# Attention maxima from q's high part alone: one 128-row product per query tile becomes two 64-row products in the two halves of TensorE's rows

## The chip, the cores and the metric

The kernel is one program on one core of a Trainium2 chip. Its engines run side by side, each with its own instruction stream in a fixed order, and they wait for each other through semaphores: TensorE (matrix products; PE in the profile, with its weight loads shown apart as PEld), VectorE (DVE), ScalarE (ACT), GpSimd (POOL) and SyncE (SP, which issues most DMAs). The metric is the device time of one execution in microseconds (us). Lower is better.

## The reference

One layer of a bidirectional hybrid encoder is applied to 2048 prompt positions and, with the same weights, to 256 sample positions (width 1024). What matters here is the attention half of the mixer: 8 query heads over 2 key/value heads, head width 64.

```
def block(qi):
    s = jnp.einsum('bqhgd,bkhd->bhgqk', qi, k).astype(jnp.float32) * scale
    p = jax.nn.softmax(s, axis=-1)
    return jnp.einsum('bhgqk,bkhd->bqhgd', p.astype(v.dtype), v)
```

q and k are RMS-normed per head and rotated before that. Next to attention there is an 8-head mLSTM (also bidirectional); then `x + [mLSTM; attention] @ w_out`, a second RMSNorm, `w_up`, a width-3 depthwise convolution, `silu(g) * a`, `w_down`, and a final RMSNorm. A softmax does not depend on the number that is subtracted from its scores, as long as it is the same for all keys of a query and near enough to their maximum that the exponentials stay in range.

## The kernel before, in words

The work runs in four phases. Phase A projects q, k, v of attention and the gates (lines 138 to 332). Then attention (`attention`, line 427) and the mLSTM (`mlstm`, line 614) run interleaved; when the mLSTM is done, the output projection (`phase_c`, line 879) takes its place beside attention. Phase D (line 1071) is the feed-forward part.

Precise products are made from pieces: a number is split into a high part (type fp32r) and the low remainder, and a product is high x high + high x low + low x high. For attention the pieces are stacked in the 128 rows (partitions) that TensorE contracts over:

- `kk` (128 rows x 512 keys): k's high part in rows 0 to 63, and the same high part once more in rows 64 to 127 (line 458 loads it twice).
- `qq` (128 rows x 512 queries): q's high part in rows 0 to 63, q's low part in rows 64 to 127.
- `kl1` (65 rows): k's low part, and a row of ones. `qm` (65 rows): q's high part, and a row that takes minus the query's maximum.

So `kk` against `qq` gives k_high x (q_high + q_low), and `kl1` against `qm` adds k_low x q_high minus the maximum.

Attention goes over 36 head blocks (`hbs`). A large one is one head and 4 tiles of 128 queries against all 2048 keys (32 of them); a small one is two heads of the sample, 4 query tiles in all against 256 keys (4 of them). For a head block:

- `prep` (488) transposes q on TensorE (L502, into `pq`) and copies it to `qq` (L504) and `qm` (L506) on ScalarE.
- `maxstep` (512) takes one query tile and 512 keys: one product into `px` (L516, 128 rows contracted, 128 queries as the stationary operand, 512 keys streaming) and a VectorE reduction over the keys into `mx` (L517). A large block needs 16 of these, a small one 4 (with 256 keys), 528 in all.
- `prep2` (519) takes the maximum over the key blocks, negates it, spreads it by four small products (`pr`, L528) and writes it into row 64 of `qm` (L530).
- `scores` (532) makes, for two key tiles of 128, the scores in `ps` (L539 and L540) and their exponentials in `pe` (L541); `values` (544) multiplies them with v two steps later (`pv`, L551).

The maxima of the next block are made during the scores of the present one: the loop at line 580 calls `maxstep` four times in each of the first four of the eight steps `kp`, then `prep2`.

`px`, `ps`, `pq` and `pr` share four PSUM banks (tag "sc", `SCB = 4`). A bank that a `px` has filled is free again when its L517 has read it, that of a `ps` when its L541 has.

The order of the instructions on each engine is not the program's order. The program hands out priorities (in the order of the text, with some stretches raised by `tc.high_priority`), `run_both` (1340) alternates between attention and the mLSTM by planned costs (the numbers that the generators yield), and a planner then simulates the program once, ahead of time, and puts on each engine, whenever it is free in the simulation, the ready instruction of the highest priority. An instruction that writes a new tile is ready only when one of the tag's banks is free in that simulation. The order that comes out is fixed in the program.

Of the kernel before, what the change touches and what calls it, by code (L numbers as in the profile page):

```python
# [9 lines left out]
F32 = mybir.dt.float32  # L10
F32R = mybir.dt.float32r
AF = mybir.ActivationFunctionType
ALU = mybir.AluOpType
AX = mybir.AxisListType
# [3 lines left out]
P = 128  # L18
# [6 lines left out]
HD = 64  # L25
# [60 lines left out]
def f32(ap):  # L86
    return ap.bitcast(F32)
# [339 lines left out]
def attention(g, tc, s1, s2, pp):  # L427


    nc = g.nc  # L430
    sp = s1
# [8 lines left out]
    def load_kv(grp, k0, k1, after=None):  # L440

        if (grp, k0) in kv:
            return
        n = k1 - k0
        sp = s2 if n == NT1 else s1
        kv[(grp, k0)] = parts = []
        for t0 in range(0, n, 4):
            m = min(4, n - t0)
            s = f"{n}_{t0}"
            kk = sp.tile([P, m * P], F32R, tag="kk" + s, name=f"kk{grp}_{s}", bufs=1)  # L450
            kl1 = sp.tile([65, m * P], F32R, tag="kl1" + s, name=f"kl1{grp}_{s}", bufs=1)
            vv = sp.tile([P, m, P], F32, tag="vv" + s, name=f"vv{grp}_{s}", bufs=1)
            c = slice((k0 + t0) * P, (k0 + t0 + m) * P)
            if after is not None:
                for t in (kk[0:1, 0:1], kk[HD:HD + 1, 0:1], kl1[0:1, 0:1], vv[0:1, 0, 0:1]):
                    nc.gpsimd.tensor_copy(t, after[0:1, 0:1])
            nc.gpsimd.memset(vv[:, :, HD:P], 1.0)
            for r in (0, HD):
                nc.gpsimd.dma_start(f32(kk[r:r + HD, :]), g.k_d[grp, 0:HD, c])
            nc.gpsimd.dma_start(f32(kl1[0:HD, :]), g.k_d[grp, HD:P, c])  # L460
            nc.gpsimd.memset(f32(kl1[64:65, :]), 1.0)
            nc.gpsimd.dma_start(vv[:, :, 0:HD], g.v_d[grp, :, k0 + t0:k0 + t0 + m])
            parts.append((kk, kl1, vv))
# [14 lines left out]
    def load_q(n):  # L478

        if n in qzs or n >= len(hbs):  # L480
            return
        t = 0
        qz = qzs[n] = sp.tile([P, 4, P], F32R, tag="qz", name=f"bq{n}", bufs=QZB)
        for h, q0, q1 in hbs[n][1]:
            nc.sync.dma_start(f32(qz[:, t:t + q1 - q0]), g.q_d[h, q0:q1].rearrange("n p d -> p n d"))
            t += q1 - q0

    def prep(n):

        s = HB()  # L490
        grp, s.qs, k0, k1 = hbs[n]
        load_q(n)
        load_q(n + 1)
        load_kv(grp, k0, k1)
        s.kv = kv[(grp, k0)]
        s.nq, s.nk = 4, k1 - k0
        s.N = s.nq * P
        s.nm = "%d_%d" % s.qs[0][0:2]
        qz = qzs.pop(n)
        pq = pp.tile([P, 512], F32R, tag="sc", name="pq" + s.nm)  # L500
        for t in range(s.nq):
            nc.tensor.transpose(pq[:, t * P:(t + 1) * P], qz[:, t, :], g.identr)  # L502
        s.qq = sp.tile([P, 512], F32R, tag="qq", name="qq" + s.nm, bufs=2)
        nc.scalar.activation(s.qq[:, 0:s.N], f32(pq[:, 0:s.N]), AF.Copy)  # L504
        s.qm = sp.tile([65, 512], F32R, tag="qm", name="qm" + s.nm, bufs=2)
        nc.scalar.activation(s.qm[0:HD, 0:s.N], f32(pq[0:HD, 0:s.N]), AF.Copy)  # L506
        s.mx = sp.tile([P, 4, 4], F32, tag="mx", name="mx" + s.nm, bufs=2)
        s.nsp = -(-s.nk * P // 512)
        s.todo = [(t, z) for z in range(s.nsp) for t in range(s.nq)]
        return s  # L510

    def maxstep(s):
        t, z0 = s.todo.pop(0)
        w = min(512, s.nk * P - z0 * 512)
        ps = pp.tile([P, 512], F32, tag="sc", name=f"px{s.nm}_{t}_{z0}")
        nc.tensor.matmul(ps[:, 0:w], s.qq[:, t * P:(t + 1) * P], s.kv[z0][0][:, 0:w], start=True, stop=True)  # L516
        nc.vector.tensor_reduce(s.mx[:, t, z0:z0 + 1], ps[:, 0:w], AX.X, ALU.max)  # L517

    def prep2(s):

        nq = s.nq
        s.m4 = sp.tile([P, 4], F32, tag="m4", name="m4" + s.nm, bufs=2)
        nc.vector.tensor_reduce(s.m4[:, 0:nq], s.mx[:, 0:nq, 0:s.nsp], AX.X, ALU.max)
        m4r = sp.tile([P, 4], F32R, tag="m4r", name="m4r" + s.nm, bufs=2)
        nc.vector.tensor_scalar(m4r[:, 0:nq], s.m4[:, 0:nq], -1.0, None, ALU.mult)
        pr = pp.tile([P, 512], F32, tag="sc", name="pr" + s.nm)
        for t in range(nq):
            nc.tensor.matmul(pr[:, t * P:(t + 1) * P], m4r[:, t:t + 1].to_broadcast([P, P]), g.identr, start=True,  # L528
                             stop=True)
        nc.scalar.activation(s.qm[HD:HD + 1, 0:s.N], pr[HD:HD + 1, 0:s.N], AF.Copy)  # L530

    def scores(s, kp):
        N = s.N
        pe = sp.tile([P, 2, 512], F32, tag="pe", name=f"pe{s.nm}_{kp}", bufs=PEB)
        for z in range(2):
            ps = pp.tile([P, 512], F32, tag="sc", name=f"ps{s.nm}_{kp}_{z}")
            kk, kl1, _ = s.kv[kp // 2]
            kc = (2 * kp + z) % 4 * P
            nc.tensor.matmul(ps[:, 0:N], kk[:, kc:kc + P], s.qq[:, 0:N], start=True, stop=False)  # L539
            nc.tensor.matmul(ps[:, 0:N], kl1[:, kc:kc + P], s.qm[:, 0:N], start=False, stop=True)  # L540
            nc.scalar.activation(pe[:, z, 0:N], ps[:, 0:N], AF.Exp)  # L541
        return kp, pe

    def values(s, kp, pe):

        N = s.N
        if kp == 0:
            s.pv = pp.tile([P, 512], F32, tag="pv", name="pv" + s.nm, bufs=1)
        for z in range(2):
            kt = 2 * kp + z  # L550
            nc.tensor.matmul(s.pv[:, 0:N], s.kv[kp // 2][2][:, kt % 4, :], pe[:, z, 0:N], start=(kt == 0),  # L551
                             stop=(kt == s.nk - 1))

    def fin1(s):

        N = s.N
        s.o1 = sp.tile([HD, 512], F32, tag="o1", name="o1" + s.nm, bufs=2)
        s.rs = sp.tile([HD, 512], F32, tag="rs", name="rs" + s.nm, bufs=1)
        nc.scalar.activation(s.o1[:, 0:N], s.pv[0:HD, 0:N], AF.Copy)
        nc.scalar.activation(s.rs[:, 0:N], s.pv[HD:P, 0:N], AF.Copy)  # L560

    def fin2(s):
        N = s.N
        nc.vector.reciprocal(s.rs[:, 0:N], s.rs[:, 0:N])
        nc.gpsimd.tensor_tensor(s.o1[:, 0:N], s.o1[:, 0:N], s.rs[:, 0:N], ALU.mult)
        for t0, (h, q0, q1) in part(s):
            r0 = HD * (h % 2)
            nc.gpsimd.dma_start(g.mix_d[q0 // 2:q1 // 2, r0:r0 + HD, 4 + h // 2].rearrange("n p t -> p n t"),
                           s.o1[:, t0 * P:(t0 + q1 - q0) * P].rearrange("p (n t) -> p n t", t=BT))
            if h == 7:  # L570
                g.mixed.update(range(q0, q1))

    cur = prep(0)
    while cur.todo:
        maxstep(cur)
        yield 0.5
    prep2(cur)
    load_kv(0, 0, NT1, cur.m4)
    old = None
    for n in range(len(hbs)):  # L580
        nxt = prep(n + 1) if n + 1 < len(hbs) else None
        nkp = cur.nk // 2
        todo = []
        for kp in range(nkp):
            todo.append(scores(cur, kp))
            if kp >= PLAG:
                values(cur, *todo.pop(0))
            if nxt is not None and nxt.todo:
                if n == len(hbs) // 2 - 1:

                    k = 2 * (kp - 2) - (nxt.nq * nxt.nsp - len(nxt.todo))
                else:
                    k = -(-len(nxt.todo) // max(nkp - kp - MXE, 1))
                for _ in range(k):
                    maxstep(nxt)
                if not nxt.todo:
                    prep2(nxt)
            if old is not None and (nxt is None or not nxt.todo or kp == nkp - 1):
                fin2(old)
                old = None  # L600
            yield 2.2
        for t in todo:
            values(cur, *t)
        fin1(cur)
        yield 1
        if nxt is not None and nxt.todo:
            while nxt.todo:
                maxstep(nxt)
            prep2(nxt)
        old, cur = cur, nxt  # L610
# [631 lines left out]
def body(tc, aps, phases="abcd"):  # L1242
# [5 lines left out]
    with ExitStack() as st:  # L1248
# [30 lines left out]
        with ExitStack() as s2:  # L1279
# [28 lines left out]
            def after_m():  # L1308
# [4 lines left out]
                return phase_c(g, g.sn, sc, pc, (sw, swo))  # L1313

            rest = run_both(g, tc, attention(g, tc, sa, sk, pa), mlstm(g, tc, g.sm, sm2, sw, g.sn, g.pj, pm), after_m)
        with ExitStack() as s2:
            s1 = pool(s2, "d_1", bufs=2)
# [105 lines left out]
```

## Time and profile before

| | us |
|---|---|
| three executions, median | 3510.44 |
| lowest and highest | 3505.19, 3514.43 |
| profiled execution, first to last instruction (span) | 3509.1 |
| TensorE busy in it | 3406.8 |
| VectorE busy | 2345.9 |
| ScalarE busy | 1683.3 |
| GpSimd busy | 1144.3 |
| px products (L516), busy time of the group | 224.5 |
| their reductions (L517), busy time of the group | 342.8 |

The profile page gives no other time of the profiled execution than its span; the span is 1.3 us under the median. In rows of the timeline the first number is the start in us from the span's start, the second is the time until the last of the merged instructions ends, and "x5" says how many were merged. A shape such as "128\*128 128x512" is that of the stationary operand (rows contracted \* columns) and of the result. Matmuls overlap each other in the pipeline, so that the duration of one is longer than the distance from its start to the next one's start.

### The profile page before, as it was taken

To read this page: it belongs to the slowest core of one execution; us is meant where nothing else is said; L and a number is where in the kernel's file an instruction comes from. 1 tells how busy PE (TensorE), PEld (TensorE's weight loads), DVE (VectorE), ACT (ScalarE), POOL (GpSimd) and SP (SyncE) were. 2 spreads that over 40 slices of the span, in tenths; PEclk is the share of its full clock that TensorE was granted. 3 is DMA by queue.
4 is the path that set the end of the run, shared out by engine and by line. 5 is a ranking of instruction groups with operands and counts; after the bars stand their busy time and mean duration, and the time that the engine had idled before them with its cause. 6 is when DMAs were issued, how large, how long until landed. Compare 5 with 4: busy or idle time off the path is not lost.

```text
span 3509.1 us, 53243 instructions
## 1 busy us (share of the span) xinstructions
PE 3406.8 (97%) x19538; PEld 3031.7 (86%) x19538; DVE 2345.9 (67%) x3962; ACT 1683.3 (48%) x3827; POOL 1144.3 (33%) x1362
## 2 busy tenths in 40 slices
PE   7889999999999999999999999999999999999998
PEld 6787787777777777767789999999999999999998
DVE  7773365546544555664444887878888879887777
ACT  5434454444444454453332544445544445655555
POOL 7863022213231322311135333224433224422222
PEclk9999999999999999999999999999999999999999
DMA  7765233233243434442247323213323213312211
GB/s 234 209 188 147 89 107 100 92 108 106 84 123 111 137 114 133 126 147 80 88 147 252 125 97 103 73 67 123 137 98 108 73 67 123 135 64 73 73 67 54
DMA packets 288917, 401.76 MB, mean 114 GB/s; under 512 B 27408, under 2 KB 188976, under 8 KB 288656
## 3 DMA queue, kind: packets, MB, share of 16 engines
q1 hardware_dynamic: 256560, 355.87, 30.9%
q0 software_dynamic: 10640, 31.86, 3.2%
q10 hardware_dynamic: 21456, 10.62, 1.0%
q8 instruction: 154, 2.52, 0.3%
q14 instruction: 107, 0.88, 0.1%
HBM read 315.55 MB, written 82.72 MB: 113 GB/s over the span
## 4 chain that ended last, share of the span: by engine, by line
PE 75%; DVE 9%; issue 5%; POOL 4%; DMA 4%; ACT 3%; SPq 0%; POOLq 0%; DVEq 0%; ACTq 0%
PE pa L1034 12%; PE pv L551 11%; PE pd L1172 11%; PE pc L1034 6%; PE po L918 5%; PE mv L668 4%; PE mj L658 4%; PE ps L539 3%; PE ps L540 3%; PE px L516 3%; PE pb L1034 3%; PE mN L794 1%; PE mj L684 1%; DVE acc L1174 1%; DVE y L1128 1%
## 5 line engine op out<-in xcount | busy, mean ns | idle before, releaser
L1172 PE MATMUL pd<-act,wd 128*128 128x384 f32 (+1 forms) x3120 | 592.0, 336 | 19.2 <-DVE acc L1174 10.8
L1172 PEld LDWEIGHTS pd<-act,wd 128*128 128x128 f32 x3120 | 540.0, 188 | 26.0 <-DVE acc L1174 14.5
L551 PE MATMUL pv<-pe,vv 128*128 128x512 f32 x1040 | 514.4, 593 | 0.2
L517 DVE TENSOR_REDUCE mx<-px 128x1 f32<-128x512 f32 (+1 forms) x528 | 342.8, 673 | 196.6 <-PE px L516 194.9
L1034 PE MATMUL pa<-nt,wut 128*128 128x386 f32 (+2 forms) x2376 | 454.7, 339 | 2.2 <-ACT u L1050 2.2
L1034 PEld LDWEIGHTS pa<-nt,wut 128*128 128x128 f32 x2376 | 422.2, 190 | 2.5 <-ACT u L1050 2.5
L541 ACT ACTIVATE pe<-ps 128x512 f32<-128x512 f32 x520 | 292.7, 595 | 266.2 <-PE ps L540 262.4
L1039 POOL TENSOR_TENSOR tw<-ru 128x512 f32<-128x512 f32 x66 | 102.1, 1547 | 740.3 <-DMA ru<-w_up 598.6
L1128 DVE SCALAR_TENSOR_TENSOR y<-u,cw,y 128x768 f32<-128x768 f32 (+1 forms) x264 | 308.9, 1171 | 35.8 <-ACT y L1121 28.8
L1174 DVE TENSOR_TENSOR acc<-pd,acc 128x384 f32<-128x384 f32 (+1 forms) x544 | 281.5, 538 | 40.1 <-PE pd L1172 38.1
L1050 ACT ACTIVATE u<-pa 128x386 f32<-128x386 f32 (+2 forms) x264 | 128.8, 488 | 328.3 <-PE pa L1034 325.8
L551 PEld LDWEIGHTS pv<-pe,vv 128*128 128x128 f32 x1040 | 189.0, 189 | 82.8 <-issue 58.3
L539 PE MATMUL ps<-qq,kk 128*128 128x512 f32 x520 | 249.5, 483 | 0.9 <-ACT pe L541 0.6
L918 PE MATMUL po<-cmx,wo 128*128 128x256 f32 x1728 | 242.5, 291 | 1.6 <-DVE wo L107 1.6
L918 PEld LDWEIGHTS po<-cmx,wo 128*128 128x128 f32 x1728 | 222.3, 191 | 24.7 <-issue 17.1
L516 PE MATMUL px<-kk,qq 128*128 128x512 f32 (+1 forms) x528 | 224.5, 455 | 2.7 <-ACT pe L541 1.3
L658 PE MATMUL mj<-mn,wm 128*128 128x256 f32 x1296 | 213.2, 305 | 8.6 <-ACT og L672 4.6
L658 PEld LDWEIGHTS mj<-mn,wm 128*128 128x128 f32 x1296 | 181.8, 194 | 38.0 <-issue 21.1
L540 PE MATMUL ps<-qm,kl 65*128 65x512 f32 x520 | 207.4, 402 | 0.1
L668 PE MATMUL mv<-wm,mn 128*128 128x256 f32 x1296 | 205.0, 298 | 0.4 <-ACT qb L664 0.4
L668 PEld LDWEIGHTS mv<-wm,mn 128*128 128x128 f32 x1296 | 178.1, 192 | 21.6 <-issue 13.9
L226 PE MATMUL pj<-w_a,n1T 128*128 128x512 f32 (+1 forms) x864 | 180.2, 363 | 8.6 <-DVE n1T L184 6.0
(285 smaller groups left out, 6663.8 us busy)
## 6 DMA issues: line engine op xcount, KB each, us to landing
ru<-w_up SPq DMA_DIRECT2D x132, 512.0 KB, 3.2
mn<-n_d SPq DMA_DIRECT2D x216, 256.0 KB, 3.3
rd<-w_down SPq DMA_DIRECT2D x66, 512.0 KB, 3.3
n_d<-n1T SPq DMA_DIRECT2D x18, 1024.0 KB, 5.2
dm<-nm_d POOLq DMA_DIRECT2D x72, 256.0 KB, 3.6
mjn<-n_d SPq DMA_DIRECT2D x72, 256.0 KB, 2.9
mvn<-n_d SPq DMA_DIRECT2D x72, 256.0 KB, 3.2
q_d<-qz SPq DMA_DIRECT2D x18, 512.0 KB, 5.6
```

What stands on the lines that cost most here:

```text
L516: nc.tensor.matmul(ps[:, 0:w], s.qq[:, t * P:(t + 1) * P], s.kv[z0][0][:, 0:w], start=True, stop=True)
L517: nc.vector.tensor_reduce(s.mx[:, t, z0:z0 + 1], ps[:, 0:w], AX.X, ALU.max)
L539: nc.tensor.matmul(ps[:, 0:N], kk[:, kc:kc + P], s.qq[:, 0:N], start=True, stop=False)
L540: nc.tensor.matmul(ps[:, 0:N], kl1[:, kc:kc + P], s.qm[:, 0:N], start=False, stop=True)
L551: nc.tensor.matmul(s.pv[:, 0:N], s.kv[kp // 2][2][:, kt % 4, :], pe[:, z, 0:N], start=(kt == 0), stop=(kt == s.nk - 1))
L658: nc.tensor.matmul(pj[:, o], s.w[c][:, a, o * P:(o + 1) * P], nT[c][:, h, :], start=(c + o + k == 0), stop=(c == NCC - 1 and k == 2 and o ...
L668: nc.tensor.matmul(pv[:, o], nT[c][:, a, o * P:(o + 1) * P], s.w[c][:, h, 256:512], start=(c + o + k == 0), stop=(c == NCC - 1 and k == 2 ...
L918: nc.tensor.matmul(po[:, o], wo[c][z // 2][:, a, n], mx[c][:, h, :], start=(c == 0 and k == 0), stop=(c == NCC - 1 and k == 2))
L1034: nc.tensor.matmul(p, w[:, aa, c, :], ops[k][:, c, bb, 0:n], start=c == 0 and i == 0 and not add, stop=c == NCC // 2 - 1 and i == 2, skip_ ...
L1128: nc.vector.scalar_tensor_tensor(y[:, s:e], u[:, s + k:e + k], cw[:, k, jj:jj + 1], y[:, s:e], ALU.mult, ALU.add)
L1172: nc.tensor.matmul(po, wds[j][c // 4][:, aa, c % 4 * P:(c % 4 + 1) * P], acts[j][:, bb, z0:z1], start=(j == 0 and k == 0), stop=(j == len( ...
L1174: nc.vector.tensor_tensor(accs[c][:, z0:z1], po, accs[c][:, z0:z1], ALU.add)
```

## The change

`maxstep` now handles two query tiles at a time. For each it contracts only 64 rows: q's high part with k's high part. The first tile uses rows 0 to 63 of `qm` and `kk`, the second rows 64 to 127 of the same tiles. For that, `qm` gets 128 rows and q's high part is copied into both halves (a second ScalarE copy per head block); row 64, which takes minus the maximum later, now holds a row of that second copy until `prep2` writes it. The two products go into two banks of the tag "sc", and each is reduced as before. The list of steps has half as many entries and the loops' counts are halved to match. The maxima leave out q_low x k_high, which they held before; the scores hold it as before.

```
-        s.qm = sp.tile([65, 512], F32R, tag="qm", name="qm" + s.nm, bufs=2)
-        nc.scalar.activation(s.qm[0:HD, 0:s.N], f32(pq[0:HD, 0:s.N]), AF.Copy)
+        s.qm = sp.tile([P, 512], F32R, tag="qm", name="qm" + s.nm, bufs=2)
+        for r in (0, HD):
+            nc.scalar.activation(s.qm[r:r + HD, 0:s.N], f32(pq[0:HD, 0:s.N]), AF.Copy)
...
-        s.todo = [(t, z) for z in range(s.nsp) for t in range(s.nq)]
+        s.todo = [(t, z) for z in range(s.nsp) for t in range(0, s.nq, 2)]
...
     def maxstep(s):
-        t, z0 = s.todo.pop(0)
+        t0, z0 = s.todo.pop(0)
         w = min(512, s.nk * P - z0 * 512)
-        ps = pp.tile([P, 512], F32, tag="sc", name=f"px{s.nm}_{t}_{z0}")
-        nc.tensor.matmul(ps[:, 0:w], s.qq[:, t * P:(t + 1) * P], s.kv[z0][0][:, 0:w], start=True, stop=True)
-        nc.vector.tensor_reduce(s.mx[:, t, z0:z0 + 1], ps[:, 0:w], AX.X, ALU.max)
+        pxs = [pp.tile([P, 512], F32, tag="sc", name=f"px{s.nm}_{t0 + i}_{z0}") for i in range(2)]
+        for i in range(2):
+            r, c = slice(HD * i, HD * i + HD), slice((t0 + i) * P, (t0 + i + 1) * P)
+            nc.tensor.matmul(pxs[i][:, 0:w], s.qm[r, c], s.kv[z0][0][r, 0:w], start=True, stop=True)
+        for i in range(2):
+            nc.vector.tensor_reduce(s.mx[:, t0 + i, z0:z0 + 1], pxs[i][:, 0:w], AX.X, ALU.max)
...
-            nc.tensor.matmul(ps[:, 0:N], kl1[:, kc:kc + P], s.qm[:, 0:N], start=False, stop=True)
+            nc.tensor.matmul(ps[:, 0:N], kl1[:, kc:kc + P], s.qm[0:HD + 1, 0:N], start=False, stop=True)
...
         maxstep(cur)
-        yield 0.5
+        yield 1
...
-                    k = 2 * (kp - 2) - (nxt.nq * nxt.nsp - len(nxt.todo))
+                    k = kp - 2 - (nxt.nq // 2 * nxt.nsp - len(nxt.todo))
```

## The prediction

> **What bounds the kernel now.** I read the page's busy shares first, then its slices, the groups of instructions, the stretch in which the maxima are made, and last the timeline of TensorE.
>
> ```profile
> PE 3406.8 (97%) x19538; PEld 3031.7 (86%) x19538; DVE 2345.9 (67%) x3962; ACT 1683.3 (48%) x3827; POOL 1144.3 (33%) x1362
> ...
> PE   7889999999999999999999999999999999999998
> ...
> L517 DVE TENSOR_REDUCE mx<-px 128x1 f32<-128x512 f32 (+1 forms) x528 | 342.8, 673 | 196.6 <-PE px L516 194.9
> ...
> L516 PE MATMUL px<-kk,qq 128*128 128x512 f32 (+1 forms) x528 | 224.5, 455 | 2.7 <-ACT pe L541 1.3
> ```
>
> The same stretch of all engines, and of L516 alone (columns: PE, PEld, DVE, ACT, POOL busy, clock, DMA share, GB/s; the second row has PE and PEld only):
>
> ```profile
> 269.00:1795.00 1526.00, 1508.70 (x8390) 1174.38 (x8391) 783.57 (x1705) 702.08 (x1925) 353.75 (x675) 1.00 0.35 109
> ```
> ```profile
> 269.00:1795.00 1526.00, 223.92 (x524) 96.98 (x524) 1.00 0.35 109
> ```
>
> TensorE is busy 1508.7 of 1526 us (98.9%) where 524 of the 528 px products lie, at full clock; VectorE is busy 51% and ScalarE 46% there. VectorE waits for px (194.9 us), px hardly for anything (2.7 us). So TensorE is the bound, and what a px product adds to or takes from TensorE's row goes to the end nearly one for one.
>
> What one px really takes is not its 455 ns; the durations overlap. The distance from start to start tells it:
>
> ```profile
> 634.20 0.39 PE L540 MATMUL ps<-qm,kl 65*128 65x512 f32 x1
> 634.43 0.39 PE L539 MATMUL ps<-qq,kk 128*128 128x512 f32 x1
> 634.66 0.40 PE L540 MATMUL ps<-qm,kl 65*128 65x512 f32 x1
> 634.89 0.40 PE L516 MATMUL px<-kk,qq 128*128 128x512 f32 x1
> 635.13 0.76 PE L658 MATMUL mj<-mn,wm 128*128 128x256 f32 x5
> 635.72 0.39 PE L516 MATMUL px<-kk,qq 128*128 128x512 f32 x1
> 635.96 0.87 PE L658 MATMUL mj<-mn,wm 128*128 128x256 f32 x6
> 636.66 0.39 PE L516 MATMUL px<-kk,qq 128*128 128x512 f32 x1
> 636.90 1.02 PE L551 MATMUL pv<-pe,vv 128*128 128x512 f32 x2
> 637.35 0.80 PE L516 MATMUL px<-kk,qq 128*128 128x512 f32 x1
> 637.99 1.02 PE L551 MATMUL pv<-pe,vv 128*128 128x512 f32 x2
> ```
>
> A px takes 0.235 us (634.89 to 635.13), with its weight load hidden behind the product before it. 512 of them at 0.235 and 16 of 256 keys at 0.12 are 122 us. No product here is shorter for having fewer rows: L540 with 65 rows takes 0.23 too. So 64 rows alone give nothing; a gain needs two products at once.
>
> These rows show a second thing: three of the four px stand alone between products of 128 rows. Over the whole trace, from the first px row to the last,
>
> ```profile
> 260.34 0.63 PE L516 MATMUL px<-kk,qq 128*128 128x256 f32 x4
> ...
> 1793.51 0.36 PE L516 MATMUL px<-kk,qq 128*128 128x256 f32 x1
> ```
>
> I count 432 unbroken runs of px in TensorE's order: 358 of one, 57 of two, 12 of three, 5 of four. Of the 264 couples that the change will put together (tiles 0 and 1, 2 and 3), only 69 are neighbours today.
>
> **The change part by part.** (1) *The two halves at once.* No row of before shows two products in different halves. At best a couple takes one product's time: -0.235 for each of 256 and -0.12 for each of 8, -61 us. If the second product can start only when its own load is through, which other loads need 0.11 us for (next fence: three loads in 0.42, of which the last takes 0.19, so (0.42 - 0.19)/2), a couple of neighbours takes 0.11 + 0.235 = 0.345 instead of 0.47, a gain of 0.125. I take the latter; at worst the couple gains nothing.
>
> (2) *Going from 128-row products to 64-row products and back.* Before has one operation whose rows are few enough to sit in one half: the 40-row transposes L378, among 128-row products.
>
> ```profile
> 247.13 1.39 PE L658 MATMUL mj<-mn,wm 128*128 128x256 f32 x10
> 248.44 0.56 PE L378 MATMUL gpt<-ident,rows 40*128 40x40 f32 x6
> 248.94 2.30 PE L658 MATMUL mj<-mn,wm 128*128 128x256 f32 x17
> 251.08 0.29 PE L297 MATMUL pk<-identr,kz 128*128 128x128 f32 x2
> 251.30 0.56 PE L378 MATMUL gpt<-ident,rows 40*128 40x40 f32 x6
> 252.21 0.56 PE L378 MATMUL gpt<-ident,rows 40*128 40x40 f32 x6 [0.35 <-DVE mt L379]
> 252.71 0.51 PE L668 MATMUL mv<-wm,mn 128*128 128x256 f32 x2
> ```
> ```profile
> 248.44 0.45 PEld L378 LDWEIGHTS gpt<-ident,rows 40*128 40x128 f32 x6
> 248.94 2.10 PEld L658 LDWEIGHTS mj<-mn,wm 128*128 128x128 f32 x17
> 250.98 0.25 PEld L297 LDWEIGHTS pk<-identr,kz 128*128 128x128 f32 x2
> ...
> 252.70 0.42 PEld L668 LDWEIGHTS mv<-wm,mn 128*128 128x128 f32 x3
> ```
> ```profile
> L516 PEld LDWEIGHTS px<-kk,qq x528: 186/190/330, 260.2 to 1793.5; 128*128 128x128 f32 x176
> ...
> L658 PE MATMUL mj<-mn,wm x1296: 274/283/687, 220.5 to 1101.3; 128*128 128x256 f32 x186
> ...
> L378 PE MATMUL gpt<-ident,rows x18: 229/230/251, 248.4 to 252.5; 40*128 40x40 f32 x18
> ```
>
> An L658 lasts 0.28 and they follow each other at (1.39 - 0.28)/9 = 0.12. *Control, no change of rows:* the run of 17 has its last start at 248.94 + 2.30 - 0.28 = 250.96; the load of L297 is issued at 250.98, 0.02 later, and hides. *In:* the run of ten has its last start at 247.13 + 1.39 - 0.28 = 248.24 and streams until 248.36; the load for L378 is issued only at 248.44, 0.20 after that start. So 0.08 to 0.10 us pass with nothing streaming, and the load, no longer hidden, follows. *Out:* the last L378 starts at 248.44 + 0.56 - 0.23 = 248.77; within their run they follow at (0.56 - 0.23)/5 = 0.07, but the next load comes at 248.94, 0.17 later: 0.10 lost. The run of 17 then needs 2.30 - 0.28 = 2.02 for 16 steps instead of 1.92: 0.10 more, the bare load. The second way out, at 252.71, shows the same 0.17 (252.21 + 0.56 - 0.23 = 252.54), and the way in at 251.30 the same 0.16 after an L297. A px has a load like L658's, so a visit to the half rows costs 0.09 + 0.10 going in and 0.10 + 0.10 coming out: **0.39 us**. The low bound is nothing (L378 is a transpose of another type, and three visits are few); the high bound is 0.39 for every px with the couple's halves also not overlapping. I take 0.39, from the only rows in which the row count changes.
>
> The Trainium skill says in TensorEngine Tiling (Array Packing), section Tiling Modes, that a change of tiling mode, unlike a change of tile, drains TensorE. By that rule there is a loss at each border; the trace agrees, with 0.08 to 0.10 us in and 0.10 out, and shows the bare load besides, which that section does not name.
>
> (3) *How many visits.* The planner hands a bank to each px separately, before and after. I infer that banks spread the px in its simulation: in the quoted rows px comes ahead of the pv that stands before it in the program, so the planner's ScalarE lags there and holds the ps banks, and px goes out one bank at a time. The change asks for two banks of the same four at once, frees them no sooner (one reduction of 673 ns each), and nothing ties the second product to the first. So I keep the order of before: 432 visits, 69 couples as neighbours. The bounds are 264 visits (each couple together) and 528 (each px alone); couples two by two would make 132.
>
> Sum of (1) to (3): 432 x 0.39 = +168, 69 x 0.125 = -9, together +160 us.
>
> (4) *The second copy into qm on ScalarE,* 36 of the same form as L506:
>
> ```profile
> L506 ACT ACTIVATE qm<-pq x36: 573/578/583, 259.8 to 1787.2; 64x512 fp32r<-64x512 f32 x36
> ```
>
> 21 us of ScalarE, which is 46% busy. Behind it in ScalarE's queue stand the exponentials L541 of the present block and the px of the next, 0.58 us later per block; TensorE has the ps and mLSTM products meanwhile. I take 0; without that cover it is at most 36 x 0.58 = 21 us. The bank of `pq` is held 0.58 us longer, in the same cover.
>
> (5) *Unchanged at 0:* the number, size and time of the reductions (528 x 673 ns; VectorE has half its time free), the halved counts of the loops (four px in each of the first four steps as before), the space (512 columns either way). `prep2`'s write into row 64 of `qm` now also follows the px that read that row, but it waits for all their maxima anyway.
>
> Forecast: 3509.1 + 160 = 3669 for the profiled execution. Its span stands 1.3 us under the median of the runs shown, so 3670.
>
> **The rivals.** *A, the couples stay together.* If both banks are mostly free at once in the planner's simulation, there are 264 visits: 264 x 0.39 - 264 x 0.125 = +70, so 3580. For it: the two products have neighbouring priorities. Against: 69 of 264 today, under the same priorities.
>
> *B, couples two by two,* as in the row `260.34 ... x4`: 132 visits are +51, and the couples save 264 x 0.125 = -33, or, if only the first load of a four is bare, 132 x (0.94 - 0.58) = -48: 3513 to 3528. Only 5 runs of four today.
>
> *C, going in and out costs nothing,* and the halves run abreast; it ends on the other side. With every couple together it is -61: 3449. With the order of before only 69 couples gain 0.235: -16, 3494. The break-even is a price per visit of 61/264 = 0.23 us with the couples together, and of 16/432 = 0.04 us with today's order. Against it: 0.39 in the rows above. The Trainium skill speaks for it in TensorE: Matmul & The Clock Gate, Part 3, section Measured speedup vs the span model: products in different row tiles start about 4 ns apart; as an estimate from that page a couple saves 0.23 us. No run here shows that, and the section says nothing on going to and fro.
>
> *D, each px pays for itself,* the second half waiting for the first: 528 x 0.39 = +206: 3716.
>
> **How the numbers follow.** Today's order with the price: 0.45, 3670 (3590 with 280 visits, 3700 with 450 at a price 0.05 higher). A: 0.20. B: 0.08, half of it within 0.3%. C: 0.18, with 0.02 of it too small to tell. D and worse: 0.09. 0.3% (11 us) is about what a measurement of this kernel can tell from no change. Slower 0.45 + 0.20 + 0.04 + 0.09 = 0.78, same 0.06, faster 0.16. The range must reach from B and the mild form of C to D: 3490 to 3720, which leaves out most of C's better form and the worst of D. The likeliest case alone: 3590 to 3700.
>
> **What would show it.** In the changed kernel's timeline: px rows of form 64\*128, most of them x1 among L658, L668 and L551; the load behind a px issued only some 0.3 us after the px's start (0.235 of streaming and the drain), not 0.02 after it; the row of 128-row products behind it 0.10 us longer than 0.12 times its count. In the stretch of the maxima TensorE stays near 99% busy and the stretch is some 160 us longer, phases A and D unchanged. Wrong: if loads of 128-row products are issued while a px streams (C), if most px rows are x2 (A) or x4 (B), or if TensorE shows new idle time before L516 (banks) or L539 (late maxima), which none of the sums holds.

## The result

The changed kernel takes 3646.76 us (median of 4, 3644.45 to 3652.75) against 3510.93 for before: 136 us more, ratio 1.0392 with a 95% interval of 1.0377 to 1.0407. The forecast was 3670 (+160), the range 3490 to 3720.

The profiled execution of the changed kernel has a span of 3642.7, 133.6 more than before's. Its page (busy shares, TensorE's slices, the groups of the maxima's reductions and products, now lines 521 and 519):

```profile
PE 3545.6 (97%) x19538; PEld 3022.2 (83%) x19538; DVE 2358.4 (65%) x3962; ACT 1707.4 (47%) x3863; POOL 1146.1 (31%) x1362
...
PE   7889999999999999999999899999999999999998
...
L521 DVE TENSOR_REDUCE mx<-px 128x1 f32<-128x512 f32 (+1 forms) x528 | 345.7, 675 | 281.3 <-PE px L519 279.4
...
L519 PE MATMUL px<-kk,qm 64*128 64x512 f32 (+1 forms) x528 | 216.5, 489 | 4.0 <-DVE mx L521 3.4
```

In the shape of a product such as `64*128 64x512` the last part gives the rows contracted and the columns that stream, not the result, which is 128 queries by 512 keys as before.

The busy time of the px group even fell (224.5 to 216.5) while its rows grew (455 to 489 ns in the mean): rows that overlap count once in it, so it does not tell what a visit costs. The added time is in the stretch of the maxima (before, then the changed kernel; columns as before):

```profile
260.00:1794.50 1534.50, 1516.97 (x8458) 1181.93 (x8457) 785.85 (x1712) 704.47 (x1931) 360.25 (x699) 1.00 0.35 110
```
```profile
259.00:1922.70 1663.70, 1654.69 (x8459) 1171.80 (x8458) 795.10 (x1713) 728.61 (x1967) 362.71 (x700) 1.00 0.33 101
```

The stretch is 129 us longer, and the last value product of attention ends at 1943.0 instead of 1813.0: 130 of the 134 us lie ahead of it. TensorE counts as busy 1654.7 of 1663.7 us (99.5%) with as many products as before (19538 in the whole kernel); the rest of the kernel is nearly unchanged (phase A's share ends at 259 against 260, and from the last value product on it takes 1699.7 against 1696.1).

The changed kernel's timeline of TensorE shows the visits. Lines 658, 551 are now 662, 555:

```profile
705.91 1.88 PE L662 MATMUL mj<-mn,wm 128*128 128x256 f32 x11
707.72 0.50 PE L519 MATMUL px<-kk,qm 64*128 64x512 f32 x1
708.15 0.38 PE L662 MATMUL mj<-mn,wm 128*128 128x256 f32 x1
708.47 0.50 PE L519 MATMUL px<-kk,qm 64*128 64x512 f32 x1
708.89 0.62 PE L662 MATMUL mj<-mn,wm 128*128 128x256 f32 x3
709.44 0.49 PE L519 MATMUL px<-kk,qm 64*128 64x512 f32 x2
709.87 1.56 PE L662 MATMUL mj<-mn,wm 128*128 128x256 f32 x11
```
```profile
281.43 0.49 PE L519 MATMUL px<-kk,qm 64*128 64x512 f32 x1
281.85 0.74 PE L672 MATMUL mv<-wm,mn 128*128 128x256 f32 x4
```
```profile
281.43 0.18 PEld L519 LDWEIGHTS px<-kk,qm 64*128 64x128 f32 x1
281.85 0.54 PEld L672 LDWEIGHTS mv<-wm,mn 128*128 128x128 f32 x4 [0.24 <-issue]
```

A lone px now takes 0.43 us from its start to the next product's (707.72 to 708.15) where it took 0.235, because its own load is bare and the next load waits: the load behind the px of 281.43 is issued at 281.85, 0.42 later. (The forecast said some 0.3; the px and its own load start together at 281.43, so that the px's record begins with a bare load, by the forecast's estimate 0.1.) So it is at all visits that end with a product of 512 keys: the next load is issued 0.426 us after the start of the last px (median of 413, the lowest 0.31), where before it was 0.003 (median of 421). The couple at 709.44 takes the same 0.43 for two.

Between products of 256 columns the three steps of a visit can be told apart (distances from start to start, medians over 127 lone px before and 93 after): from the product before to the px 0.118 before and 0.209 after, from the px to the next product 0.232 and 0.428, from that to the one behind it 0.117 and 0.222. Over all three steps a lone px takes 0.467 before and 0.859 after, 0.392 more; a couple, of which there are only six and four in this surrounding, 0.698 and 0.86, so 0.16 more.

By my count of the timeline there are 423 unbroken runs of px (340 of one, 65 of two, 14 of three, 4 of four), 72 of 264 couples are neighbours, and 78 products start within 20 ns of the one before them, in the other half.

### The profile page after: what moved, and what is told of

Its sections match the earlier page's. It is cut to its first block, busy times and chain, and to the rows that moved or that the text cites. A ratio compares the mean times of both kernels' runs of the same rounds, so it can differ in the third digit from the quotient of the medians.

```text
span 3642.7 us, 53286 instructions
## 1 busy us (share of the span) xinstructions
PE 3545.6 (97%) x19538; PEld 3022.2 (83%) x19538; DVE 2358.4 (65%) x3962; ACT 1707.4 (47%) x3863; POOL 1146.1 (31%) x1362
## 5 line engine op out<-in xcount | busy, mean ns | idle before, releaser
L555 PE MATMUL pv<-pe,vv 128*128 128x512 f32 x1040 | 532.5, 610 | 0.0
L555 PEld LDWEIGHTS pv<-pe,vv 128*128 128x128 f32 x1040 | 176.2, 189 | 105.0 <-issue 87.4
L519 PE MATMUL px<-kk,qm 64*128 64x512 f32 (+1 forms) x528 | 216.5, 489 | 4.0 <-DVE mx L521 3.4
L672 PE MATMUL mv<-wm,mn 128*128 128x256 f32 x1296 | 216.2, 306 | 0.2 <-ACT qb L668 0.2
```

The costliest lines, as they stand in the source:

```text
L519: nc.tensor.matmul(pxs[i][:, 0:w], s.qm[r, c], s.kv[z0][0][r, 0:w], start=True, stop=True)
L672: nc.tensor.matmul(pv[:, o], nT[c][:, a, o * P:(o + 1) * P], s.w[c][:, h, 256:512], start=(c + o + k == 0), stop=(c == NCC - 1 and k == 2 ...
```

## The experiments

The theory was that a visit to the half rows costs about 0.39 us and neighbours in two halves save something. The main rival was that the couples (two banks at once), the second copy or the new order cost the time, and not the row count.

**1. Only the row count.** The kernel before, with one edit:

```
-        nc.tensor.matmul(ps[:, 0:w], s.qq[:, t * P:(t + 1) * P], s.kv[z0][0][:, 0:w], start=True, stop=True)
+        nc.tensor.matmul(ps[:, 0:w], s.qq[0:HD, t * P:(t + 1) * P], s.kv[z0][0][0:HD, 0:w], start=True, stop=True)
```

> The kernel before, with one line changed: each maxima product contracts rows 0 to 63 alone (q's high part against k's high part), still one query tile at a time, one bank each, no second copy; the planned order of TensorE differs from before's in a handful of places, with 431 unbroken runs of these products. Theory (going from 128-row products to 64-row products and back costs 0.39 us a visit): 431 x 0.39 = +168 us, less up to 10 us of waits that it covers, so 3669 to 3679 us, ratio 1.045 to 1.048. Rival (the 136 us of the changed kernel come from asking for two banks at once, from the second copy, or from the new planned order, not from the row count): within 0.3% of before, 3500 to 3522 us.

Measured: 3667.54 us, ratio 1.0444 (1.0430 to 1.0458), +156 us. The rival falls: no couple, no copy, the same order but for 10 of 19538 places, and yet slower than the changed kernel. The same place in the timeline before, and in this run:

```profile
280.21 0.52 PE L668 MATMUL mv<-wm,mn 128*128 128x256 f32 x3
280.56 0.39 PE L516 MATMUL px<-kk,qq 128*128 128x512 f32 x1
280.80 0.51 PE L668 MATMUL mv<-wm,mn 128*128 128x256 f32 x3
281.15 0.39 PE L516 MATMUL px<-kk,qq 128*128 128x512 f32 x1
```
```profile
277.88 0.52 PE L668 MATMUL mv<-wm,mn 128*128 128x256 f32 x3
278.33 0.50 PE L516 MATMUL px<-kk,qq 64*128 64x512 f32 x1
278.76 0.62 PE L668 MATMUL mv<-wm,mn 128*128 128x256 f32 x3
279.31 0.50 PE L516 MATMUL px<-kk,qq 64*128 64x512 f32 x1
```

From px to px 0.59 before and 0.98 here: 0.39 for a visit. As both kernels have the same 19538 products in almost the same order, I laid the distances from start to start side by side: the steps next to a px grew by some 162 us in all, which is 0.376 for each of the 431 visits, and the others shrank by some 6 us, which I take for waits that the longer visits cover. (By how the few places of another order are counted, the first sum is 160 to 165 and the second 6 to 8.) That is why 156 came out and not 168.

**2. One row more.** `s.qq[0:HD + 1, ...]` and `kk[0:HD + 1, ...]` in the same place: 65 rows.

> As the run with 64 rows, but 65 rows are contracted (one row of q's low part comes along), so that the product no longer fits one half of TensorE's rows; the planned order is that of before on every engine. Theory (it is the change between half and full rows that costs): within 0.3% of before, 3500 to 3522 us. Rival (short products as such, or their weight loads with fewer rows, are what hinders the overlap): as slow as the 64-row run, about 3670 us.

Measured: 3516.87 us, ratio 1.0015 (1.0006 to 1.0024). It is within the 0.3% that were expected, and 151 us faster than with one row less. The three steps of a visit between products of 256 columns take 0.118, 0.235 and 0.119 here, as before, and 0.209, 0.428 and 0.222 in the run with 64 rows. A contraction shorter than 128 rows as such thus costs next to nothing; the price comes in between 65 and 64 rows, where the product fits a half.

**3. Couples in one half.** The changed kernel with both tiles in rows 0 to 63:

```
-            r, c = slice(HD * i, HD * i + HD), slice((t0 + i) * P, (t0 + i + 1) * P)
+            r, c = slice(0, HD), slice((t0 + i) * P, (t0 + i + 1) * P)
```

> The changed kernel, with both query tiles of a couple in rows 0 to 63 (couples, banks, copies and nearly the order kept; 422 visits). The trace of the changed kernel has 78 products that start within 20 ns of the one before, in the other half. Theory (neighbours in two halves run fully abreast, each such product saves its 0.235 us): slower than the changed kernel by 78 x 0.235 = 18 us, 3665 us, ratio to before 1.0445. Rival 1 (the second half starts only after its own load, a couple saves 0.125): 78 x 0.125 = 10 us slower, 3657 us, ratio 1.042. Rival 2 (the halves take turns, the same starts are only how the profile records them): as the changed kernel, 3647 us, ratio 1.039.

Measured: 3656.94 us, ratio 1.0417 (1.0403 to 1.0431), 10 us over the changed kernel. That is rival 1's number, but the two ratios' intervals leave room for 2 to 16 us, and the couple at the same place of this run says otherwise:

```profile
711.83 0.62 PE L662 MATMUL mj<-mn,wm 128*128 128x256 f32 x3
712.38 0.73 PE L519 MATMUL px<-kk,qm 64*128 64x512 f32 x2
713.03 1.56 PE L662 MATMUL mj<-mn,wm 128*128 128x256 f32 x11
```

0.65 us from 712.38 to 713.03 against 0.43 in two halves: 0.22 saved, not 0.125. With 78 such products the time alone could not decide it; experiment 5 has 251.

**4. Couples with 128 rows.** The changed kernel, its two banks at once and its second copy kept, with `s.qq[:, c]` and all rows of `kk`:

> The changed kernel with its couples, two banks at once and second copy, but each product contracts all 128 rows of q's high and low part as before (435 unbroken runs planned). Theory (only the row count matters): within 0.5% of before, 3494 to 3528 us, the second copy and the banks at 0. Rival (banks or the copy cost): up to 21 us for the copy, 3532 us, or about the changed kernel's 3647 us if the banks are the cause.

Measured: 3512.50 us, ratio 1.0008 (0.9999 to 1.0017). Couples, banks and the second copy together cost nothing that can be measured.

**5. Couples kept together.** All tiles of the tag "sc" become two banks wide, two instead of four, so that a couple becomes ready as one:

```
-        pxs = [pp.tile([P, 512], F32, tag="sc", name=f"px{s.nm}_{t0 + i}_{z0}") for i in range(2)]
+        px2 = pp.tile([P, 2, 512], F32, tag="sc", name=f"px{s.nm}_{t0}_{z0}")
+        pxs = [px2[:, i] for i in range(2)]
...
+        ps2 = pp.tile([P, 2, 512], F32, tag="sc", name=f"ps{s.nm}_{kp}")
         for z in range(2):
-            ps = pp.tile([P, 512], F32, tag="sc", name=f"ps{s.nm}_{kp}_{z}")
+            ps = ps2[:, z]
...
-            pa = pool(s2, "b_p", bufs=SCB, space=PSUM)
+            pa = pool(s2, "b_p", bufs=SCB // 2, space=PSUM)
```

`pq` and `pr` take the first half of such a tile. It was run with 128-row products, with 64-row products in the two halves, and with 64-row products in one half.

> The kernel before, with all tiles of the tag 'sc' made two banks wide (two of them instead of four single banks), so that the two products of a couple become ready together; each contracts 128 rows of q's high and low part; scores of two key tiles share one tile; the second copy into qm is made. 267 unbroken runs of maxima products are planned. It is the measure for the next run. Both theories: no slower than 1.5% over before, 3511 to 3565 us, from banks that come free in twos.

> As the two-bank run, with 64-row products in the two halves: 267 visits planned, about 250 couples as neighbours. Theory 1 (0.376 us a visit, the average that the 64-row run showed, and abreast couples save 0.235 each): 267 x 0.376 - 250 x 0.235 = +42 us over the two-bank run with 128 rows. Theory 2 (0.376 a visit, couples save 0.125, the second load being bare): 267 x 0.376 - 250 x 0.125 = +69 us. Against the changed kernel both say a clear gain: about 90 us or 65 us less, before the cost of the wide banks.

> As the two-bank run with 64-row products, but both products of a couple use rows 0 to 63 (266 visits, the same order but for a few places). What the two halves give by themselves. Theory 1 (abreast): 250 x 0.235 = 59 us slower than with two halves. Theory 2 (second load bare): 31 us slower. A third (the halves take turns): no slower.

Measured: 3590.54 (1.0220, 1.0205 to 1.0235), 3631.02 (1.0332, 1.0315 to 1.0350) and 3685.62 us (1.0487, 1.0469 to 1.0505). The wide banks cost 78 us, more than the 1.5% that I had allowed; what makes up the 78 us was not taken apart. With them, half rows in two halves cost 40 us more (theory 1: 42, theory 2: 69), and one half 55 us more than two (theory 1: 59, theory 2: 31). The ratios' intervals leave each of these differences about 9 us either way, which excludes theory 2. The rows agree: between products of 256 columns the three steps of a couple take 0.696 with 128 rows (37 couples), 0.864 in two halves (39) and 1.09 in one half (40), so 0.23 saved. So neighbours in two halves run fully abreast. I count 269 visits to half rows in the run with two halves, the two of L378 among them, and 251 products abreast. Against the changed kernel it gains only 16 us, since the banks take back most.

The count also answers for the planner: with the banks handed out in twos the runs of px fell from 423 to 267. That the couples come apart where each product gets a bank of its own, and stay together where they share a tile, is thus shown. Why the banks come free singly in the planner's simulation was not looked at.

**6. Four products a visit.** On the wide banks, all four query tiles of a key block are issued as one unbroken unit, which needs both wide tiles at once:

```
+        px = [pp.tile([P, 2, 512], F32, tag="sc", name=f"px{s.nm}_{t0}_{z0}") for t0 in (0, 2)]
+        with tc.tile_critical():
+            for t in range(4):
+                r, c = slice(HD * (t % 2), HD * (t % 2) + HD), slice(t * P, (t + 1) * P)
+                nc.tensor.matmul(px[t // 2][:, t % 2, 0:w], s.qm[r, c], s.kv[z0][0][r, 0:w], start=True, stop=True)
```

That is the form with two halves; the one with 128 rows has `s.qq[:, c]` and all rows of `kk` there.

> The two-bank run with 128-row products, with all four query tiles of a key block issued as one unbroken group of four products (131 groups planned), which needs all four banks at once. It is the measure for the next run. Expected 1 to 4% over before, 3545 to 3650 us: TensorE's scores have to wait for banks until the reductions (two of 0.68 us for each wide bank) are through.

> The same groups of four with 64-row products in two halves, in the same order on every engine: 131 visits, each with two couples. Theory 1 (0.376 us a visit, the average of the first 64-row run, and four products take the time of two): 131 x (0.376 - 0.47) = -12 us, just faster than the same groups with 128 rows. Theory 2 (a couple saves 0.125): 131 x (0.376 - 0.25) = +17 us, slower. It tells whether two couples a visit pay for the way in and out.

Measured: 4126.70 us with 128 rows (1.1760, 1.1743 to 1.1778) and 4070.37 with two halves (1.1606, 1.1575 to 1.1637). Both expectations missed, the first by far. The groups are as planned, but each has idle time before it; first 128 rows, then two halves:

```profile
603.81 1.02 PE L557 MATMUL pv<-pe,vv 128*128 128x512 f32 x2
605.29 1.21 PE L520 MATMUL px<-kk,qq 128*128 128x512 f32 x4 [0.46 <-issue]
606.59 0.71 PE L788 MATMUL mI<-C,qb 128*128 128x130 f32 x4
```
```profile
596.40 1.02 PE L557 MATMUL pv<-pe,vv 128*128 128x512 f32 x2
597.85 0.73 PE L520 MATMUL px<-kk,qm 64*128 64x512 f32 x4 [0.43 <-issue]
598.67 0.71 PE L788 MATMUL mI<-C,qb 128*128 128x130 f32 x4
```

In the stretch of the maxima TensorE is busy 1812.4 of 2141 us (85%) with the 128-row groups, at a granted clock of 0.89 (0.88 in the run with halves), against 1.00 before. What of the 616 us comes from the unbroken unit, what from needing all four banks and what from the lower clock was not separated. The two runs still tell something between them: the group takes 1.30 us to the next start with 128 rows and 0.82 in halves, 0.48 less (0.46 in the median of the 126 groups of 512 keys), about the whole 0.47 that two couples can save. In time the 131 unbroken groups gave 56 us, 0.43 each, with room for about 0.1 either way. So little of the price of a visit is left. In both runs each of these 126 groups has idle time of TensorE before it, and all but two behind it: nothing streams that would have to run dry, and the loads are bare with 128 rows too. That this is the reason is read from the rows; no run tests it alone.

## Why the prediction was right

The mechanism was right, and the sum too high in two of its terms, both the same way.

*TensorE as the bound* held: 98.9% busy became 99.5%, and the time went to the end nearly one for one. Of what the visits added, some 6 us went into waits that existed before (experiment 1).

*The price of a visit, 0.39 us from the 40-row transposes,* held in the rows to the hundredth (0.392 between products of 256 columns), and in its parts: 0.09 for running dry on the way in, 0.20 at the px for its bare load and the way out, 0.10 for the bare load behind it were forecast, and the three steps grew by 0.091, 0.196 and 0.105. Experiments 1 and 2 show the cause: 64 rows against 65. The base was narrow: the prediction counts three visits in its rows, but the six transposes at 252.21 follow the six at 251.30 with a wait and no other product between them, so there are two. That they price a px of another type so closely could not be known ahead. Averaged over all surroundings it is 0.376, and counted in the kernel's time, each against its own 128-row twin, 156/431 = 0.36 (experiment 1), 144/422 = 0.34 (experiment 3 against 4) and 95/266 = 0.36 (the one-half and 128-row runs of experiment 5). The step that was a little too dear is thus the term 432 x 0.39 = 168: the visits came to 423, and each was worth 0.36 and not 0.39 at the end.

*The number of visits, from today's order,* held: 423 for 432, 72 neighbouring couples for 69. Of the reason that I gave, experiment 5 shows that a bank for each product keeps the couples apart; that ScalarE lags in the planner's simulation and holds the banks stays inferred.

*The two halves at once* was sized too small. I took 0.125 for a neighbouring couple, with the second load bare; the changed kernel shows 0.235, since the second product starts 3 to 4 ns after the first. The Trainium skill gives about 4 ns for each further tile that runs abreast (TensorE: Matmul & The Clock Gate, Part 3, section Measured speedup vs the span model). The trace agrees, with these 3 to 4 ns. With 78 such products it is 78 x 0.235 = 18 us instead of 9. With both corrections: 423 x 0.376 - 18 - 6 = 135 against 136 measured.

*The second copy, the banks and the counts at 0* held, taken together: experiment 4.

*The rivals.* A (couples together) came in experiment 5: on the forecast's own terms +70, measured +40 over its twin, because of the 0.235. C (no price) is excluded by experiment 1, the mild form as well. B (four a visit) did not occur in the changed kernel, with 4 runs of four, and as experiment 6 builds it it comes with wide gaps. D (each px for itself) did not occur. No version here beats the kernel before: at 0.36 a visit and 0.235 a couple, one couple a visit loses, and two couples a visit (0.47) would gain only 131 x 0.11 = 14 us if the banks for it cost nothing. That last is worked out, not run.

## What to carry to other kernels

A product that uses half of TensorE's rows does not mix freely with full ones: at each border TensorE's row runs dry and the weight load stands bare, here 0.39 us for the way in and out together, against the 0.235 us that a second product of 512 columns abreast saves. So count the borders in the planned order, not the products; the order is set by what hands out the banks, and neighbours in the program need not be neighbours on the engine. A few odd visits of another operation in the old trace (here 18 small transposes in two visits) can price such a border before anything is built.

## What was not expected of the hardware

- 64 rows and 65 rows differ by 151 us in the same kernel, in nearly the same order (3667.54 and 3516.87).
- Two products in the two halves start 3 to 4 ns apart and take the time of one (0.43 us for a couple as for a lone px), though each has its own weight load; in one half the couple takes 0.65.
- The border costs little where TensorE has idle time at it anyway: 0.47 - 0.43 = 0.04 us a visit in experiment 6, with room for about 0.1 either way, against 0.36 in a busy row.
